# Values of heads 0 and 1 made together, with 512 moving columns and a new order

## The chip, the cores and the metric

The kernel runs on one core of a Trainium2 chip. Its metric is the device time of one execution in microseconds (us). Five engines work side by side, each through its own instructions in order: PE (TensorE, matrix products; PEld is its weight load), DVE (VectorE), ACT (ScalarE), POOL (GpSimd) and SP (SyncE, which here issues all DMA transfers).

## What is computed

One layer of an encoder trunk on 1024 tokens with 1024 features, float32. Only the start matters here: a norm, one input projection, and gated linear attention with four heads in both directions.

```python
h = rmsnorm(x, norm_mix)                       # x: (1024 tokens, 1024 features)
q, k, v, r, lr_f, lr_b, u, g_a, g_b = split(h @ w_in)
                                               # q, k: 4 heads of 128; v: 4 heads of 256
log_a = log_sigmoid(lr @ w_decay_up + b_decay) / 16        # one for each direction
# per head, in chunks: decayed keys and queries, scores inside a chunk times v,
# and a state S = decay * S + k^T v carried from chunk to chunk, forward and backward
o = gla(q, k, v, log_a_f) + gla_backward(q, k, v, log_a_b)
...                                            # norm per head, gates, pooling, merge, FFN, norm
```

## The kernel before

**Products in three parts.** Every float32 operand of the large products is split into a high part and a rest: `split_to` (L196) copies the source to the high part on ACT (L197) and subtracts it on DVE or POOL (L198). `mm3` (L273) then issues three matmuls (high by high, high by rest, rest by high) into one PSUM bank and calls `pump`. A step of `mm3` with 512 moving columns counts as one unit, one with 256 as half a unit.

**What is interleaved, and how.** The order of all instructions is fixed while the program is written, and `pump` (L158) is the clock of that: generators wait in the list `side`, and each `pump` takes the units from the first of them and runs its next step when its delay is used up. So a generator's instructions come between two products of the main line, at a place set by counted units and not by time. `pending` holds weight splits (one for every two units), and `aside` holds jobs that prepare later weights (`prepare_beside`, one job for every so many units, POOL operations with DMA transfers).

**The main line of the first 390 us.** Tokens are in eight tiles of 128. `norm_x` norms a tile and then issues the load of the tile four ahead; `to_features` transposes two tiles on PE (L318), applies the gain on ACT (L325, tile `hh`) and takes the rest on DVE (L328, `hl`). `values(w, v, t)` (L384) makes the values of one head for one token tile: the token tile is the stationary operand, the 256 columns of the weights move, 24 matmuls. Before, the values of head 0 for all eight tiles come first, with the norms and transposes of the later tiles between them; then the low-rank product for the decays (L449) for both token halves; then queries and keys of head 0 (`project_qk`, four products of eight units, weights stationary, 512 tokens moving); then, for heads 1 to 3, queries and keys and after them the values of eight tiles (32 units each). After head 3 comes the section that makes `r` (L996 on), 128 units.

**Attention beside it.** `attention(h)` is a generator that is put in line once the head's queries and keys are made, and it runs beside the next products. Its steps, with delays in units, are: four decay products `z` (L641), Exp and Ln on ACT (L650, L656); then four times a decay (DVE: L663 `la`, a scan L670 or L675, L678/L671, L681), its exponentials (ACT, L688 to L690) and its application to the keys (DVE L696, POOL L697 and L698), 4.4 units apart; key transposes `kp` (L714), split into `kt` by ACT and DVE; then seven backward state updates `advance` 1.2 units apart (PE `kv`, DVE `st` L726 or L728, DVE `so` L733, ACT `sb` L780); scores (L741); and eight output steps with the forward state. The fourth update of the backward chain still uses the first `kt`; the fifth is the first that needs the second one. The generator of the next head starts when the one before it has ended; an attention is 59 to 60 units long. `normalize` (L834) scales the outputs of the head before, eight DVE operations after the Exps of the next head.

**Buffers.** 39 slots of one tile size in SBUF are shared by nearly everything; PSUM has three banks for the main products and five for the rest. Raw weights have four buffers.

Of the kernel before, what the change touches and what calls it, by code (L numbers as in the profile page):

```python
# [17 lines left out]
P = 128  # L18
# [33 lines left out]
def kernel(  # L52
# [38 lines left out]
    def name(s):  # L91
        count[0] += 1
        return f"{s}_{count[0]}"
# [92 lines left out]
    def begin(gen, delay=0.0):  # L186
        side.append([gen, delay])
# [47 lines left out]
    order = []  # L235
    for h in range(HEADS):
        cols_of = [(Q0 + h * DK, DK), (K0 + h * DK, DK), (V0 + h * DV, DV)]
        order += [(w_in, KT, *c) for c in (cols_of if h else cols_of[2:] + cols_of[:2])]
    order += [(w_in, KT, R0 + j * P, P) for j in range(KT)]
    order = iter(order)  # L240
    loaded, ready = [], []
# [72 lines left out]
    def transpose_tile(ps, xt, i, kp):  # L314
        for kk in range(2):
            c = slice((2 * kk + i) * P, (2 * kk + i + 1) * P)
            k = 2 * kp + kk
            nc.tensor.transpose(ps[:, c], xt[:, k * P : (k + 1) * P], ident[:, :])  # L318

    def gain_and_split(ps, kp, t0, act, gain):  # L320
        c = slice((t0 % 4) * P, (t0 % 4 + 2) * P)
        both = range(2 * kp, 2 * kp + 2)
        srcs = [(ps[:, i * 2 * P : (i + 1) * 2 * P], gain[:, k : k + 1]) for i, k in enumerate(both)]
        for k, (src, g) in zip(both, srcs):
            nc.scalar.activation(act(k, t0 // 4)[0][:, c], src, AF.Copy, scale=g)  # L325
        for k, (src, g) in zip(both, srcs):
            hi, lo = act(k, t0 // 4)
            nc.vector.scalar_tensor_tensor(  # L328
                lo[:, c], src, g, as_f32(hi[:, c]), op0=ALU.mult, op1=ALU.subtract
            )  # L330
# [19 lines left out]
    def load_x(t):  # L350
        nc.sync.dma_start(xt[t % 4][:, :], x[t * P : (t + 1) * P, :])
# [4 lines left out]
    def load_up(i, d, w):  # L356
        r = 2 * RANK * i + RANK * d
        nc.sync.dma_start(uraw[r : r + RANK, :, d, :], w[0].rearrange("r (h c) -> r h c", h=HEADS))

    load_x(0)  # L360
    load_rows(0, *vec_rows[0])
    load_x(1)
    for i in range(1, len(vec_rows)):
        load_rows(sum(n for _, n in vec_rows[:i]), *vec_rows[i])
    fetch()
    for t in (2, 3):
        load_x(t)
    nc.sync.dma_start(lraw[:, :, :], w_in[:, LR0:U0].rearrange("(k p) c -> p k c", p=P))
# [35 lines left out]
    def value_slots():  # L404
        return [(slot(F32R, (4, DV), "vh"), slot(F32R, (4, DV), "vl")) for _ in range(2)]

    v = value_slots()
    norm_x(0)

    vps = bank(ps_g, "vps")  # L410
# [7 lines left out]
    for t in range(2):  # L418
        for kp, ps in enumerate(trs):
            transpose_tile(ps, xn[t], t, kp)  # L420
    prepare()
    for kp, ps in enumerate(trs):
        pending.pop(0)()
        gain_and_split(ps, kp, 0, hT, g_mix)
    w = take(ahead=False)
    norm_x(2)
    norm_x(3)
    for t in range(0, NT, 2):
        if t + 4 < NT:
            begin(norms(t + 4), 1)  # L430
        if t == 2:
            for d, w_up in enumerate((w_decay_up_fwd, w_decay_up_bwd)):
                for i in range(4):
                    load_up(i, d, w_up)
        values(w, v, t)
        finish_side()
        if t + 2 < NT:
            begin(to_features(xn[(t + 2) % 4 :], t + 2, hT, g_mix), 0.5)
        values(w, v, t + 1)
        finish_side()  # L440
        if t == 4:
            low_rank_weights()
    prepare()
    lrT = slot(F32R, (2, HALF), "lrT")
    for half in range(2):
        ps = bank(ps_mm)
        for k in range(KT):
            for i in range(2):
                nc.tensor.matmul(  # L449
                    ps[:, :], lw[k // 4][:, k % 4, :, :].rearrange("p a r -> p (a r)"), hT(k, half)[i],  # L450
                    start=k == 0 and i == 0, stop=k == KT - 1 and i == 1,
                )
            pump(2 / 3)
        nc.scalar.copy(lrT[:, half, :], ps[:, :])
        nc.vector.tensor_tensor(lrT[64:96, half, :], ps[64:96, :], as_f32(lrT[64:96, half, :]), op=ALU.subtract)
# [175 lines left out]
    def attention(h, q, k):  # L631


        qe = [slot(s="qe") for _ in range(2)]
        ke = [slot(s="ke") for _ in range(2)]
        fac = {}
        runs = ((1, 1), (0, 1), (0, 0), (1, 0))
        zs, las = {}, {}
# [43 lines left out]
            totals[half, d] = tot  # L682

        def exponentials(half, d):
            cs, tot, e_q = zs[half, d], totals[half, d], qe[half]
            f = vec(12, "fac")
            sign = INV_NORMALIZER if d == 0 else -INV_NORMALIZER
            nc.scalar.activation(e_q[:, d, :], cs[:, :], AF.Exp, scale=sign)  # L688
            nc.scalar.activation(cs[:, :], cs[:, :], AF.Exp, scale=-sign)
            nc.scalar.activation(f[:, :8], tot[:, :], AF.Exp, scale=INV_NORMALIZER)  # L690
            fac[half, d] = f

        def apply_decay(half, d):
            f, e_q, e_k = fac[half, d], qe[half], ke[half]
            f2 = f[:, :8].rearrange("p (n a) -> p n a", a=2)
            nc.vector.tensor_tensor(e_k[:, d, :], zs[half, d][:, :], k[:, half, :], op=ALU.mult)  # L696
            nc.gpsimd.tensor_tensor(e_q[:, d, :], e_q[:, d, :], q[:, half, :], op=ALU.mult)  # L697
            nc.gpsimd.tensor_tensor(f[:, 8:], f2[:, :, 0], f2[:, :, 1], op=ALU.mult)  # L698
# [146 lines left out]
    def load_o(h):  # L845
        o_heads[h] = [slot(shape=(4, DV), s="ol") for _ in range(2)]
        for half in range(2):
            nc.sync.dma_start(o_heads[h][half][:, :, :], o_out[h][:, 4 * half : 4 * half + 4, :])

    for h in range(HEADS):  # L850
        qk = project_qk()
        begin(attention(h, *qk))
        if h == 0:
            prepare_beside(map(branch_jobs, range(4)), 6)
        if h > 0:
            v = value_slots()
            w = take()
            for t in range(NT):
                values(w, v, t)
        v_heads[h] = v  # L860

    class Unit:

# [1006 lines left out]
```

## Time and profile before

| | us |
|---|---|
| timed runs, median of 3 | 1399.0 (1397.69 to 1401.03) |
| the profiled execution, its span | 1400.4 |
| PE busy in it | 1371.4 (98%) |
| DVE / ACT / POOL busy | 854.4 / 624.6 / 750.4 |

The profile gives no time of its own for the profiled execution beside its span; its span lies within the range of the timed runs, 1.4 us above their median. The lines of the profile name the kernel's lines (L271 is the matmul in `products`), and an operation is written as output tile <- input tiles; the moving operand of a matmul stands first. "Idle before" is the time for which the engine had nothing to do just before an instruction, with what it waited for.

### The profile page before, as it was taken

The numbers are of one execution on the slowest core, as the hardware profiler recorded it, in microseconds if no ns is written. First come the engines' busy times: TensorE is split into PE (matmuls) and PEld (weight loads), VectorE is DVE, ScalarE is ACT, GpSimd is POOL, SyncE is SP. The second block draws the span as 40 slices with busy tenths as digits, with TensorE's granted clock in tenths as the row PEclk, the third lists the DMA queues.
The fourth block names the chain that finished last, engine by engine and source line by source line (L and its number), as shares of the span: only waits on it lengthen the run. The fifth ranks groups of instructions, "written<-read, shape, count | busy, mean of one in ns | idle before, by whom it ended". The sixth has DMA issues, their size and how long they took to land.

```text
span 1400.4 us, 18571 instructions
## 1 busy us (share of the span) xinstructions
PE 1371.4 (98%) x6677; PEld 1157.4 (83%) x6677; DVE 854.4 (61%) x1073; ACT 624.6 (45%) x1119; POOL 750.4 (54%) x558
## 2 busy tenths in 40 slices
PE   7999999999999999999999999999999999999997
PEld 6889898988888878788887888888888888888876
DVE  6256857677745975587874865556565556343363
ACT  6364655554334444455346633333333334453253
POOL 3251616132288456468665176666666667454354
PEclk9999999999999999999999999999999999999999
DMA  6212413222368667996524455554444447975461
GB/s 193 76 45 61 136 59 107 89 79 71 125 207 286 199 220 235 346 407 233 194 76 173 173 180 174 173 173 156 145 142 148 140 153 255 388 255 218 165 234 67
DMA packets 167612, 243.62 MB, mean 174 GB/s; under 512 B 10936, under 2 KB 98016, under 8 KB 167520
## 3 DMA queue, kind: packets, MB, share of 16 engines
q1 hardware_dynamic: 167520, 242.45, 51.2%
q8 instruction: 52, 0.85, 0.2%
q14 instruction: 40, 0.33, 0.1%
HBM read 164.55 MB, written 77.86 MB: 173 GB/s over the span
## 4 chain that ended last, share of the span: by engine, by line
PE 81%; DVE 7%; ACT 4%; issue 3%; POOL 2%; DMA 2%; SPq 0%; POOLq 0%; DVEq 0%; ACTq 0%
PE ps L271 73%; PE op L813 2%; POOL wl L198 1%; PE kv L271 1%; PE sc L741 1%; PE op L271 1%; DVE z L670 1%; PE yb L271 1%; PE tr L318 1%; PE ps L449 1%; PE tp L972 1%; DMA gor<-g_out 0%; DMA wor<-t_out 0%; DVE z L675 0%; DMA u_out<-uph 0%
## 5 line engine op out<-in xcount | busy, mean ns | idle before, releaser
L198 POOL TENSOR_TENSOR wl<-fs,wh 128x512 fp32r<-128x512 f32 x120 | 165.9, 1386 | 163.4 <-ACT wh L197 138.1
L271 PE MATMUL ps<-gl,wh 128*128 128x512 f32 x616 | 239.8, 389 | 0.9 <-DVE gl L1462 0.9
L271 PE MATMUL ps<-gh,wh 128*128 128x512 f32 x616 | 240.4, 390 | 0.0
L271 PE MATMUL ps<-gh,wl 128*128 128x512 f32 x616 | 239.7, 389 | 0.0
L198 POOL TENSOR_TENSOR wl<-fraw,wh 128x512 fp32r<-128x512 f32 x90 | 129.1, 1435 | 63.9 <-ACT wh L197 63.9
L271 PE MATMUL ps<-hh,wh 128*128 128x512 f32 x376 | 150.4, 400 | 0.0
L198 POOL TENSOR_TENSOR ol<-gor,oh 128x1024 fp32r<-128x1024 f32 (+1 forms) x42 | 100.3, 2394 | 93.1 <-ACT oh L197 86.0
L271 PE MATMUL ps<-hh,wl 128*128 128x512 f32 x376 | 146.9, 391 | 0.0
L271 PE MATMUL ps<-hl,wh 128*128 128x512 f32 x376 | 146.8, 390 | 0.0
L198 POOL TENSOR_TENSOR wl<-raw,wh 128x512 fp32r<-128x512 f32 x47 | 64.4, 1382 | 152.8 <-ACT wh L197 141.4
L271 PEld LDWEIGHTS ps<-gl,wh 128*128 128x128 f32 x616 | 115.7, 188 | 25.0 <-DVE gl L1462 1.3
L271 PEld LDWEIGHTS ps<-gh,wl 128*128 128x128 f32 x616 | 115.7, 188 | 24.2
L271 PEld LDWEIGHTS ps<-gh,wh 128*128 128x128 f32 x616 | 115.7, 188 | 23.6
L271 PE MATMUL ps<-oh,oh 128*128 128x512 f32 x308 | 119.9, 389 | 1.3 <-DVE x L1792 1.3
L271 PE MATMUL ps<-ol,oh 128*128 128x512 f32 x308 | 119.9, 389 | 0.2 <-DVE ol L198 0.2
L271 PE MATMUL ps<-oh,ol 128*128 128x512 f32 x308 | 119.8, 389 | 0.0
L198 POOL TENSOR_TENSOR wl<-wraw,wh 128x512 fp32r<-128x512 f32 x56 | 90.9, 1653 | 45.4 <-ACT wh L197 36.1
L198 DVE TENSOR_TENSOR ol<-wor,oh 128x1024 fp32r<-128x1024 f32 (+1 forms) x42 | 62.0, 1496 | 53.9 <-ACT oh L197 46.6
L197 ACT CAST wh<-fs 128x512 fp32r<-128x512 f32 x120 | 73.8, 615 | 28.4 <-DVE fs L882 28.3
L271 PEld LDWEIGHTS ps<-hh,wl 128*128 128x128 f32 x376 | 70.8, 188 | 15.3
L271 PEld LDWEIGHTS ps<-hl,wh 128*128 128x128 f32 x376 | 71.1, 189 | 13.5
L271 PEld LDWEIGHTS ps<-hh,wh 128*128 128x128 f32 x376 | 71.1, 189 | 13.2
(251 smaller groups left out, 3197.4 us busy)
## 6 DMA issues: line engine op xcount, KB each, us to landing
fraw<-in_w_ffn_in_dram SPq DMA_DIRECT2D x44, 512.0 KB, 6.1
gor<-g_out SPq DMA_DIRECT2D x35, 512.0 KB, 6.3
raw<-in_w_in_dram SPq DMA_DIRECT2D x48, 256.0 KB, 3.1
g_out<-s SPq DMA_DIRECT2D x44, 256.0 KB, 2.3
fraw<-in_w_in_dram SPq DMA_DIRECT2D x20, 512.0 KB, 6.5
wor<-t_out SPq DMA_DIRECT2D x20, 512.0 KB
g_out<-g SPq DMA_DIRECT2D x33, 256.0 KB, 2.6
x<-in_x_dram SPq DMA_DIRECT2D x16, 512.0 KB, 4.9
```

The costliest lines, as they stand in the source:

```text
L197: nc.scalar.copy(hi, src)
L198: eng.tensor_tensor(lo, src, as_f32(hi), op=ALU.subtract)
L271: nc.tensor.matmul(ps, a[i], b[j], start=first and n == 0, stop=last and n == 2, skip_group_check=onto)
L318: nc.tensor.transpose(ps[:, c], xt[:, k * P : (k + 1) * P], ident[:, :])
L449: nc.tensor.matmul(ps[:, :], lw[k // 4][:, k % 4, :, :].rearrange("p a r -> p (a r)"), hT(k, half)[i], start=k == 0 and i == 0, stop=k == ...
L670: nc.vector.tensor_tensor_scan(cs[:, :], cy, la[:, :], 0.0, op0=ALU.mult, op1=ALU.add)
L741: nc.tensor.matmul(sc[d][:, i * CH : (i + 1) * CH], chunk_of(ke, n, d), chunk_of(qe, n, d), start=True, stop=True,)
L813: nc.tensor.matmul(op[:, :DV], a, b, start=False, stop=j == len(terms) - 1)
L972: nc.tensor.transpose(tp[:, i * P : (i + 1) * P], o_heads[j // 2][half][:, i, (j % 2) * P : (j % 2 + 1) * P], ident[:, :],)
```

## The change

Three things change together.

1. The values of heads 0 and 1 are made in one product of 512 moving columns (256 for each head) by `pair_products`, for which 8 weight tiles of 128 rows by 512 columns are loaded one at a time (`load_pair_weight`) and kept split in slots (`split_pair_weight`, ACT with DVE and POOL in turn). Before, the weights of one head were four transfers of 256 rows by 256 columns.
2. The order is new. Tiles 0 and 1 come first, both within each step over the features; their steps also issue the splits of the weights, the gains and the norms of tiles 2 and 3 (`first_steps`). Then tile 2, tile 3, and head 0's queries and keys by token halves (`first_qk`): low-rank product, queries and keys for the first half, while the tiles of the second half are normed and transposed, then the same for the second. Then `attention(0)` is put in line, and tiles 4, 5 and (6, 7) follow beside it. Head 1 has no values of its own any more. Heads 2 and 3 are as before.
3. The slots `qe` and `ke` of an attention are taken when they are first written, and the jobs beside the products come every 5 units and not every 6, beginning 32 units later.

In PE's program there are 192 matmuls fewer; from the last part of the `r` section on, the order of PE's instructions is the same as before.

```diff
-        order += [(w_in, KT, *c) for c in (cols_of if h else cols_of[2:] + cols_of[:2])]
+        order += [(w_in, KT, *c) for c in cols_of[: 2 if h < 2 else 3]]
...
+    def load_pair_weight():
+        k = len(pair_raw)
+        raw = wts.tile([P, HALF], F32, tag="raw", name=name("vraw"), bufs=4)
+        nc.sync.dma_start(raw[:, :], w_in[k * P : (k + 1) * P, V0 : V0 + 2 * DV])
+        pair_raw.append(raw)
+
+    def split_pair_weight():
+        k = len(pair_w)
+        w = slot(F32R, s="wv")
+        pair_w.append((w[:, 0, :], w[:, 1, :]))
+        split_to(*pair_w[k], pair_raw[k][:, :], (nc.vector, nc.gpsimd)[k % 2])
+        if len(pair_raw) < KT:
+            load_pair_weight()
...
-    fetch()
+    for _ in range(4):
+        load_pair_weight()
     for t in (2, 3):
         load_x(t)
...
+    def pair_products(ts, before=None):
+        banks = [bank(ps_mm) for _ in ts]
+        for k in range(KT):
+            if before:
+                before(k)
+            for ps, t in zip(banks, ts):
+                mm3(ps[:, :], tokens(hT(k, t // 4), t), pair_w[k], k == 0, k == KT - 1)
+        for ps, t in zip(banks, ts):
+            for h in range(2):
+                if t % 4 == 0:
+                    pair_v[h].append((slot(F32R, (4, DV), "vh"), slot(F32R, (4, DV), "vl")))
+                split_to(*(part[:, t % 4, :] for part in pair_v[h][t // 4]), ps[:, h * DV : (h + 1) * DV])
+
+    def first_steps(k):
+        if k % 2 == 0:
+            gain_and_split(trs[k // 2], k // 2, 0, hT, g_mix)
+        if k < KT - 1:
+            split_pair_weight()
+        if k in (3, 5):
+            norm_x(k // 2 + 1)
+        if k == 6:
+            begin(to_features(xn[2:], 2, hT, g_mix), 0.5)
+
+    split_pair_weight()
+    pair_products((0, 1), first_steps)
+    finish_side()
+    fetch()
+    begin(norms(4), 1)
...
+    pair_products((2,))
+    finish_side()
+    begin(to_features(xn, 4, hT, g_mix), 1)
+    low_rank_weights()
     prepare()
-    for kp, ps in enumerate(trs):
...
-    w = take(ahead=False)
-    norm_x(2)
-    norm_x(3)
-    for t in range(0, NT, 2):
...
-        values(w, v, t)
...
+    pair_products((3,))
+    finish_side()
...
+    def first_qk():
+        q, k = slot(s="q"), slot(s="k")
+        begin(norms(6), 1)
+        low_rank(0)
+        weights = [take()]
+        begin(to_features(xn[2:], 6, hT, g_mix), 1)
+        for half in range(2):
+            if half:
+                finish_side()
+                low_rank(1)
+                prepare()
+            for n, (dst, scale) in enumerate(((q, DK**-0.5), (k, 1.0))):
+                if n == len(weights):
+                    weights.append(take(ahead=False))
+                ps = feature_major(weights[n], hT, half)
+                nc.scalar.activation(dst[:, half, :], ps[:, :], AF.Copy, scale=scale)
+        return q, k
+
     for h in range(HEADS):
-        qk = project_qk()
+        qk = project_qk() if h else first_qk()
         begin(attention(h, *qk))
         if h == 0:
-            prepare_beside(map(branch_jobs, range(4)), 6)
-        if h > 0:
+            for ts in ((4,), (5,), (6, 7)):
+                pair_products(ts)
+            v_heads.update(enumerate(pair_v))
+            prepare_beside(map(branch_jobs, range(4)), 5)
+        if h > 1:
             v = value_slots()
             w = take()
             for t in range(NT):
                 values(w, v, t)
-        v_heads[h] = v
+            v_heads[h] = v
```

More of the change, by code (lines that the diff above doesn't have):

```diff
@@ L358, in load_up @@
         nc.sync.dma_start(uraw[r : r + RANK, :, d, :], w[0].rearrange("r (h c) -> r h c", h=HEADS))
+    pair_raw, pair_w = [], []
+    def load_pair_weight():
[10 more added lines that the diff above has]
+            load_pair_weight()
     load_x(0)
@@ L405, in value_slots @@
         return [(slot(F32R, (4, DV), "vh"), slot(F32R, (4, DV), "vl")) for _ in range(2)]
-    v = value_slots()
     norm_x(0)
@@ L420, with low_rank @@
             transpose_tile(ps, xn[t], t, kp)
-    prepare()
-    for kp, ps in enumerate(trs):
-        pending.pop(0)()
-        gain_and_split(ps, kp, 0, hT, g_mix)
-    w = take(ahead=False)
-    norm_x(2)
-    norm_x(3)
-    for t in range(0, NT, 2):
[L429 to L434, printed above, removed]
-        values(w, v, t)
[L436 to L443, printed above, removed]
+    pair_v = [[], []]
+    def pair_products(ts, before=None):
[24 more added lines that the diff above has]
+    begin(norms(4), 1)
+    for d, w_up in enumerate((w_decay_up_fwd, w_decay_up_bwd)):
+        for i in range(4):
+            load_up(i, d, w_up)
+    pair_products((2,))
+    finish_side()
+    begin(to_features(xn, 4, hT, g_mix), 1)
+    low_rank_weights()
+    prepare()
+    pair_products((3,))
+    finish_side()
     lrT = slot(F32R, (2, HALF), "lrT")
-    for half in range(2):
+    def low_rank(half):
         ps = bank(ps_mm)
@@ L631, in attention @@
     def attention(h, q, k):
-        qe = [slot(s="qe") for _ in range(2)]
-        ke = [slot(s="ke") for _ in range(2)]
+        qe, ke = {}, {}
         fac = {}
@@ L684, in exponentials @@
         def exponentials(half, d):
+            if half not in qe:
+                qe[half] = slot(s="qe")
             cs, tot, e_q = zs[half, d], totals[half, d], qe[half]
@@ L693, in apply_decay @@
         def apply_decay(half, d):
+            if half not in ke:
+                ke[half] = slot(s="ke")
             f, e_q, e_k = fac[half, d], qe[half], ke[half]
```

## The prediction

> **What bounds the kernel now.** I read the page first: the span, PE's share, and the chain of work that ended last.
>
> ```profile
> span 1400.4 us, 18571 instructions
> PE 1371.4 (98%) x6677; PEld 1157.4 (83%) x6677; DVE 854.4 (61%) x1073; ACT 624.6 (45%) x1119; POOL 750.4 (54%) x558
> PE 81%; DVE 7%; ACT 4%; issue 3%; POOL 2%; DMA 2%; SPq 0%; POOLq 0%; DVEq 0%; ACTq 0%
> ```
>
> PE is the bound. A change in PE's own work counts in full; anything else counts where PE waits for it. So I go through the stretch that the diff touches, up to the `r` section, and look for PE's work there and for its waits. The PE work is read from the chain of waits in order of time (start, us, how many):
>
> ```profile
> 24.04 3.59 PE ps L271 x30
> 27.63 0.44 PE tr L318 x4
> 45.08 7.28 PE ps L449 x32
> 52.36 22.44 PE ps L271 x99
> ```
>
> 30 matmuls of 256 columns took 3.59 us, 119.7 ns each; 99 of 512 took 22.44 us, 226.7 ns each. From 24.04 us PE runs without a break until head 0's attention begins at 52.36 + 22.44 = 74.8 us. What is left at 24.04 us confirms it: 3 matmuls of tile 1 and 6 tiles of 24 (147 x 0.1197 = 17.6), 8 groups of transposes (3.5), the low-rank product (7.28), queries and keys (22.44), together 50.8 us.
>
> **Columns.** 384 matmuls of 256 columns become 192 of 512: 192 x (2 x 119.7 - 226.7) ns = 2.4 us less PE work, half of it ahead of head 0's attention and half beside it. The Trainium skill, "TensorE: Matmul & The Clock Gate", Back-to-back issue gap, gives N/2.4 + 2.5 ns for a warm matmul; by that 256 columns take 109.2 ns and 512 take 215.8 ns, and the estimate from it would be a gain of 0.5 us alone. The trace has 119.7 and 226.7, 11 ns more for each instruction, and decides.
>
> **The start.** Views: the timeline by engine, and the windows (PE, PEld, DVE, ACT, POOL busy, granted clock, DMA share, GB/s).
>
> ```profile
> 8.72 10.19 SPq L351 DMA_DIRECT2D x<-in_x_dram  x4
> 17.96 1.06 ACT L311 ACTIVATE xn<-x 128x1024 f32<-128x1024 f32 x1 [0.15 <-DMA x<-in_x_dram]
> 3.00:4.00 1.00, 0.00 (x0) 0.00 (x0) 1.00 (x3) 0.00 (x0) 0.90 (x2) 1.00 0.99 361
> 12.99 0.65 ACT L197 CAST wh<-raw 128x512 fp32r<-128x512 f32 x1
> 13.50 0.88 ACT L325 ACTIVATE hh<-tr,cols 128x256 fp32r<-128x256 f32 x2
> 14.23 1.10 ACT L311 ACTIVATE xn<-x 128x1024 f32<-128x1024 f32 x1
> 15.27 1.09 ACT L311 ACTIVATE xn<-x 128x1024 f32<-128x1024 f32 x1
> 15.45 0.15 DVE L302 TENSOR_SCALAR n1rs<-n1ms 128x1 f32<-128x1 f32 x1 [0.16 <-ACT xn L311]
> 16.27 0.75 DVE L307 TENSOR_SCALAR xn<-x,n1rs 128x1024 f32<-128x1024 f32 x1 [0.66 <-POOL n1rs L303]
> 14.42 0.88 DVE L328 SCALAR_TENSOR_TENSOR hl<-tr,cols,hh 128x256 fp32r<-128x256 f32 x2 [0.37 <-ACT hh L325]
> 11.22 3.79 POOL L198 TENSOR_TENSOR wl<-raw,wh 128x512 fp32r<-128x512 f32 x3 [2.99 <-ACT wh L197]
> 10.69 0.56 PE L271 MATMUL ps<-wh,hh 128*128 128x256 f32 x1
> ```
>
> The first pair (tiles 0 and 1) now wants 2 MB of weights instead of 1 MB. Four of its eight tiles take the places of the old four transfers. The fifth waits for a raw buffer, and in SP's order it stands behind the loads of token tiles 4 and 5 (issued 8.72 us on). Tile 5 landed at 17.9 us (ACT then stopped waiting for it), so the fifth weight tile comes 256 KB / 361 GB/s = 0.7 us later: 18.7 us. The next three follow every 0.7 us, ahead of their use. Token tiles 6 and 7 and head 0's weights come behind them, some 15 us before they are needed: nothing.
>
> Before that PE has four steps of 6 matmuls, 5.4 us of work, from 10.7 us on and partly at a low clock: done at about 17.2. Then, in ACT's order: cast at 18.7, the square of tile 2 at 19.2 (casts start 0.51 apart, squares 1.04), gains at 20.25. PE's fifth step begins at 20.8. Its third matmul wants `hl`, which on DVE stands behind the norm of tile 2: the sum of squares is there at 20.4, `xn` starts 0.8 later and takes 0.75, half of the `hl` pair 0.45: 22.45 us. From there PE has 22 matmuls (5.0) and four groups of transposes (1.8): it would be done at 29.2 at full clock. POOL's splits (1.3 each) and the second norm stay just ahead of it. The clock:
>
> ```profile
> 12.77:16.18 3.41, 2.95 (x20) 2.43 (x20) 1.93 (x6) 3.41 (x7) 2.73 (x3) 1.00 1.06 350
> 16.18:19.59 3.41, 1.57 (x12) 1.24 (x12) 1.99 (x5) 3.05 (x8) 1.16 (x3) 1.00 0.48 149
> 19.59:23.00 3.41, 3.41 (x19) 3.41 (x17) 2.75 (x8) 1.62 (x5) 0.55 (x1) 0.50 0.73 229
> 227.80:231.20 3.40, 1.31 (x6) 0.84 (x6) 2.15 (x3) 2.59 (x6) 2.55 (x3) 1.00 0.29 77
> 231.20:234.60 3.40, 3.20 (x11) 2.81 (x12) 3.23 (x6) 1.02 (x2) 3.32 (x4) 0.50 0.20 77
> ```
>
> A stretch of 3.4 us in which PE was busy for 1.57 or 1.31 us is followed by one at clock 0.50; one with 2.95 is not. With the same stretches, the changed start has 1.0 busy in 16.18 to 19.59 and about 1.4 in the next: half clock to 26.4 us. That takes 2.0 us: done at 31.2. I take this; 29.2 is the low end. Then follow 48 matmuls (10.9), transposes (3.5), the low-rank product, queries and keys: 44.1 us. Two norm chains are now close behind PE. Tiles 6 and 7 are squared only when tile 3's values are cast, and two squares (2.1), scaling (0.8 + 0.75, partly twice) and casts make about 5 us, while PE has the low-rank half and one step, 4.3 us: 0.7 us of waiting (0 to 1.5). Head 0's attention begins at 31.2 + 44.1 + 0.7 = 76.0 us, **1.2 us later** than before (73.3 to 77: 1.5 earlier to 2.2 later), its share of the 2.4 us included.
>
> **Beside the attention.** Tiles 4 to 7 take 96 x 226.7 ns = 21.8 us where 192 x 119.7 ns = 23.0 stood: **-1.2 us**. What else changes is which products lie beside which step. PE's waits of that stretch, and DVE's and ACT's rows that lead to them:
>
> ```profile
> 95.85 0.69 DVE L198 TENSOR_TENSOR kt<-kp,kt 128x512 fp32r<-128x512 f32 x1 [1.98 <-ACT kt L197]
> 103.72 0.69 DVE L198 TENSOR_TENSOR kt<-kp,kt 128x512 fp32r<-128x512 f32 x1 [1.15 <-ACT kt L197]
> 104.32 0.41 DVE L198 TENSOR_TENSOR vl<-ps,vh 128x256 fp32r<-128x256 f32 x1
> 104.73 0.28 PE L271 MATMUL kv<-vh,kt 128*128 128x256 f32 x1
> 146.07 0.69 DVE L663 TENSOR_TENSOR la<-la,z 128x512 f32<-128x512 f32 x1 [1.85 <-ACT z L656]
> 164.62 0.69 DVE L198 TENSOR_TENSOR kt<-kp,kt 128x512 fp32r<-128x512 f32 x1 [0.64 <-ACT kt L197]
> 166.72 0.28 PE L271 MATMUL kv<-vh,kt 128*128 128x256 f32 x1
> 206.85 2.05 ACT L656 ACTIVATE z<-z 128x512 f32<-128x512 f32 x4
> 209.23 0.42 DVE L198 TENSOR_TENSOR vl<-ps,vh 128x256 fp32r<-128x256 f32 x1 [3.23 <-ACT vh L197]
> 209.57 0.68 DVE L663 TENSOR_TENSOR la<-la,z 128x512 f32<-128x512 f32 x1
> 227.99 0.38 PE L271 MATMUL kv<-vh,kt 128*128 128x256 f32 x1 [0.25 <-DVE st L726]
> 231.40 0.58 PE L271 MATMUL kv<-vh,kt 128*128 128x256 f32 x1 [2.10 <-DVE kt L198]
> 295.75 0.39 PE L271 MATMUL kv<-vh,kt 128*128 128x256 f32 x1 [1.04 <-DVE kt L198]
> ```
>
> In each head the fifth state update is the first to need the second `kt`. In head 0 it was ready at 104.4 for 104.73, 0.3 to spare; in head 1 at 165.3 for 166.72, 1.4 to spare. In heads 2 and 3 PE waited for it.
>
> *Head 2.* DVE could have begun its first decay with the first Ln, at 207.5; it stood for 3.23 us before the rest of the last value tile (209.23), whose cast ACT had behind all four Ln. In head 1 nothing stood there. The price: 0.25 + 2.10 us, and then 3.4 us at half clock, 1.7: 4.0 us. Now head 1's attention is put in line only at unit 64 and not at 32, so it starts 4 to 6 units later than the end of head 0's would let it, and all later ones move with it. In the program's order head 2's attention now has no value split between its Exps and its first decay, as head 1's had none: **-4.0 us** (0 if the scans, not the split, made the lag).
>
> *Head 0.* New in DVE's order: two splits (tile 5) behind the first decay, and four (tiles 6 and 7) between the fourth decay and the first state update. DVE had 1.98 us idle ahead of the first `kt`, which covers the two. The four take 4 x 0.41 = 1.6 us and delay the second `kt`; between the first key transposes and the fifth update stand 33 matmuls of 512 where 9 of 512 and 48 of 256 stood, 7.5 us for 7.8, so PE comes 0.3 earlier: 1.6 + 0.3 - 0.3 = **+1.6 us**. A wait of that size leaves 1.8 us busy, between the 1.57 that brought a half clock and the 2.95 that didn't; with it 3.3 to 4.0, and 0 if scans run freer while fewer weights are split beside them.
>
> *Head 1* lies as head 0 did, against the values of head 2: 0. *Head 3* still has one value tile behind its Ln, where before there were two; of its 1.04 us I take off half: **-0.5** (-1.0 to +3.0, head 2's price before).
>
> `qe` and `ke` taken later cost nothing: the slots they now take were last read by the first steps of the last pair, units earlier. From the last part of `r` on PE's order is unchanged, and the gain is carried on.
>
> **Sum:** 1.2 - 1.2 - 4.0 + 1.6 - 0.5 = -2.9 us. Against the profiled execution, 1400.4, that is 1397.5; it lies 1.4 above the median of the runs, 1399.0, which gives **1396.1 us**. About 2.8 us (0.2%) is what a measurement here can tell from no change, so the forecast lies at that bound.
>
> **Rivals.**
> *The wait moves from head 2 to head 0.* The four splits bring the whole wait with the half clock there, 4.0 instead of 1.6: -0.5 us, 1398.5. For it: `kt` had only 0.3 us to spare. Against: tile 5's splits are covered, and few weights are split on POOL then.
>
> *The scans decide, and it gets slower.* How long a scan takes varies by a factor of two:
>
> ```profile
> L675 DVE TENSOR_TENSOR_SCAN z<-la,carry x8: 1229/1670/2341, 85.2 to 280.6; 128x511 f32<-128x511 f32 x8
> L670 DVE TENSOR_TENSOR_SCAN z<-carry,la x8: 1231/1776/2277, 91.4 to 289.7; 128x512 f32<-128x512 bf16 x8
> ```
>
> The branch jobs now come every 5 units and not every 6, so POOL works more beside these heads. If that stretches the four scans of a head by more than 0.35 us each (1.4 to spare in head 1; from 1.7 to over 2.0 us), PE waits there. Head 2 then keeps its 4.0 and head 0 gets 4.0: 1.2 - 1.2 + 4.0 - 0.5 = +3.5, 1402.5; head 1 as well, 1406.5. The Trainium skill, "SBUF — State Buffer", Who interferes with whom, has a VectorE instruction with two SBUF inputs shut out while GpSimd reads SBUF; for the scans, whose result lies in PSUM, the spread of 1.23 to 2.34 us agrees.
>
> *No half clock in the start* is the low end above: 2.0 us less, 1394.1. That the change doesn't do what it says is no rival: PE's program has 192 matmuls fewer.
>
> **How the numbers follow.** The forecast has 0.53 (its own range 1392.5 to 1399, with the start at either clock and head 0 from 0 to 3.3), the moved wait 0.25, the scans 0.22. The forecast case is faster by over 0.2% in about eight of ten, the moved wait rarely, the scans never: faster 0.47. Within 0.2%: most of the moved wait and some of the forecast, 0.28. Slower: the scans and a rest, 0.25. The range 1392.0 to 1403.0 takes the forecast's own and the scans with two heads.
>
> **What would show it.** PE idle from about 17 to 21 us with ACT's cast of the fifth weight tile starting at 18.7; the granted clock 0.50 in one or two stretches behind it; the first `z` at 76; no PE wait over 0.5 us for `kt` in head 2, one of 1 to 2 us in head 0. Wrong would be: a first `z` past 78, a wait for `kt` in head 1, or head 2's wait unchanged although no value split stands ahead of its first decay.

## The result: slower by 0.4%, and the profile after

| | median, us | runs | lowest to highest |
|---|---|---|---|
| before | 1399.37 | 6 | 1397.69 to 1402.18 |
| after | 1404.13 | 6 | 1403.81 to 1406.19 |

The ratio is 1.0043 with a 95% interval of 1.0028 to 1.0058: 4.8 us slower. The forecast was 1396.1 us, with a range up to 1403.0. It was wrong in sign, and the time lies outside the range.

The page of the changed kernel's profiled execution (this run took 1404.11 us, 1.7 more than its span):

```profile
span 1402.4 us, 18182 instructions
PE 1367.1 (97%) x6485; PEld 1143.3 (82%) x6485; DVE 857.7 (61%) x1076; ACT 624.6 (45%) x1119; POOL 744.3 (53%) x555
```

PE has 192 instructions and 4.3 us of busy time less, but the span is 2.0 us longer: what was taken out of PE's work came back as waiting. Two rows of PE's timeline in each kernel, the first `z` of head 0 and the first `tp` of the `r` section, behind which PE's order is the same in both, cut the span into three. After, then before:

```profile
77.67 0.39 PE L674 MATMUL z<-lrT,up 128*128 128x512 f32 x1
337.74 0.49 PE L1030 MATMUL tp<-ident,ol 128*128 128x128 f32 x3
```

```profile
74.64 0.39 PE L641 MATMUL z<-lrT,up 128*128 128x512 f32 x1
```

| | before | after | difference | forecast |
|---|---|---|---|---|
| up to the first `z` | 74.6 | 77.7 | +3.0 | +1.2 |
| from there to the first `tp` (334.1 before) | 259.4 | 260.1 | +0.6 | -4.1 |
| the rest | 1066.3 | 1064.7 | -1.7 | 0 |

The last row is no work of the change: before, one stretch of 3.4 us at clock 0.50 lay at 569 us, where the changed kernel's execution has none.

The start, in windows (us, PE, PEld, DVE, ACT, POOL busy, granted clock, DMA share, GB/s), and the rows of the timeline at the end of PE's hole:

```profile
14.80:18.21 3.41, 1.86 (x9) 1.20 (x7) 0.00 (x0) 0.00 (x0) 0.00 (x0) 1.00 1.01 384
18.21:21.63 3.42, 0.73 (x2) 0.30 (x2) 1.57 (x4) 3.24 (x7) 0.82 (x2) 1.00 0.09 32
21.63:25.04 3.41, 2.94 (x7) 2.38 (x8) 2.74 (x7) 2.45 (x6) 2.60 (x3) 0.50 0.50 154
```

```profile
18.39 0.62 ACT L197 CAST wv<-vraw 128x512 fp32r<-128x512 f32 x1 [5.60 <-DMA vraw<-in_w_in_dram]
20.47 0.73 PE L271 MATMUL ps<-wv,hh 128*128 128x512 f32 x2 [3.81 <-ACT hh L325]
36.98 0.44 PE L318 MATMUL tr<-ident,xn 128*128 128x128 f32 x2 [0.28 <-DVE n1rs L302]
38.46 0.44 PE L318 MATMUL tr<-ident,xn 128*128 128x128 f32 x2 [1.04 <-DVE xn L307]
50.63 0.44 PE L318 MATMUL tr<-ident,xn 128*128 128x128 f32 x2 [1.06 <-DVE xn L307]
```

The cast of the fifth weight tile and the hole came nearly as foretold (18.7 and 17.2 to 20.8 us), with one stretch at half clock behind it. The last three rows were not: PE also waits for the norms of tiles 4 and 5 (1.3 us), and of 6 and 7 (1.1 us, ending at 50.6). That is 2.4 us of idle time, 2.7 counted from start to start of the matmuls, where the forecast had 0.7.

PE's waits between 80 and 330 us, grouped by what it waited for (total, times, longest), after and then before:

```profile
PE kv L271 <- DVE kt L198: 3.7, 3, 1.4
PE kv L271 <- ACT vh L197: 1.9, 1, 1.9
PE op L271 <- DVE p L198: 0.2, 1, 0.2
```

```profile
PE kv L271 <- DVE kt L198: 3.4, 3, 2.1
PE kv L271 <- DVE st L726: 0.2, 1, 0.2
PE op L271 <- DVE p L198: 0.2, 1, 0.2
```

The rows behind these, one for each of heads 0, 1 and 2:

```profile
104.27 0.38 PE L271 MATMUL kv<-vh,kt 128*128 128x256 f32 x1 [1.92 <-ACT vh L197]
175.95 0.39 PE L271 MATMUL kv<-vh,kt 128*128 128x256 f32 x1 [1.42 <-DVE kt L198]
240.07 0.39 PE L271 MATMUL kv<-vh,kt 128*128 128x256 f32 x1 [1.20 <-DVE kt L198]
```

Before, heads 0 and 1 had no such wait. Head 2's got shorter, but did not go; head 3's is as before (1.06 us, 1.04 before). The expectations below count a wait from start to start of two matmuls beyond their pitch (2.08, 1.58, 1.36), which is about 0.16 more than the idle time in a row.

### The profile page after: what moved, and what is told of

Its sections match the earlier page's. It is cut to its first block, busy times and chain, and to the rows that moved or that the text cites. A ratio compares the mean times of both kernels' runs of the same rounds, so it can differ in the third digit from the quotient of the medians.

```text
span 1402.4 us, 18182 instructions
## 1 busy us (share of the span) xinstructions
PE 1367.1 (97%) x6485; PEld 1143.3 (82%) x6485; DVE 857.7 (61%) x1076; ACT 624.6 (45%) x1119; POOL 744.3 (53%) x555
## 5 line engine op out<-in xcount | busy, mean ns | idle before, releaser
L198 POOL TENSOR_TENSOR wl<-raw,wh 128x512 fp32r<-128x512 f32 x40 | 54.4, 1370 | 129.5 <-ACT wh L197 119.1
```

Of the source, the lines that this page charges most:

```text
L198: eng.tensor_tensor(lo, src, as_f32(hi), op=ALU.subtract)
```

## The experiments

Each is the changed kernel with one edit, unless it says otherwise. All times, with the ratio to the kernel before in runs on the same chip, and the median of the kernel before in those runs:

| | median, us | lowest to highest | ratio | 95% interval | kernel before, us |
|---|---|---|---|---|---|
| loads of tiles 4 and 5 later (e_start) | 1400.42 | 1398.44 to 1403.13 | 1.0016 | 1.0003 to 1.0028 | 1398.70 |
| norms earlier (e_norms) | 1401.55 | 1400.29 to 1404.06 | 1.0025 | 1.0013 to 1.0037 | 1398.70 |
| stores of outputs later (e_flush) | 1401.77 | 1400.46 to 1402.78 | 1.0020 | 1.0007 to 1.0032 | 1398.70 |
| tiles in the order 4, 7, 6, 5 (e_order0) | 1403.58 | 1402.85 to 1406.74 | 1.0039 | 1.0027 to 1.0052 | 1398.70 |
| 256 columns again (e_c256) | 1403.45 | 1402.18 to 1406.31 | 1.0032 | 1.0020 to 1.0044 | 1399.52 |
| jobs every 6 units (e_every6) | 1409.06 | 1406.37 to 1411.18 | 1.0068 | 1.0049 to 1.0086 | 1399.52 |
| the first three together (all3) | 1393.88 | 1392.62 to 1395.26 | 0.9959 | 0.9946 to 0.9973 | 1399.52 |
| and tile 4 ahead (all3_t4) | 1392.79 | 1390.86 to 1394.23 | 0.9951 | 0.9937 to 0.9965 | 1399.52 |
| and tiles 4, 5 ahead (all3_t45) | 1390.69 | 1389.26 to 1391.72 | 0.9946 | 0.9934 to 0.9959 | 1398.65 |
| all3_t4 with 256 columns (all3_t4_c256) | 1396.49 | 1394.73 to 1397.51 | 0.9986 | 0.9977 to 0.9995 | 1398.65 |
| the kernel before, stores later (before_flush) | 1397.07 | 1394.87 to 1398.28 | 0.9986 | 0.9977 to 0.9995 | 1398.65 |

The changed kernel's 1404.13 us stands against 1399.37 for the kernel before. The times below come from three chips, on which the kernel before differs by up to 0.9 us; so a gain against the changed kernel is given as the difference of the two medians, and in brackets as the difference of their distances to the kernel before. A ratio has an interval of about 1.7 us to either side, so a gain under about 2 us is not shown by the times alone.

### The hole in the start

```diff
 def norm_x(t):
-        if t + 4 < NT:
+        if 2 <= t and t + 4 < NT:
             load_x(t + 4)
 def split_pair_weight():
         if len(pair_raw) < KT:
             load_pair_weight()
+            if len(pair_raw) == KT:
+                load_x(4)
+                load_x(5)
```

> The changed kernel with one difference: the loads of token tiles 4 and 5 are issued behind the eighth weight tile and not ahead of the fifth. Theory A (the order of the transfers makes the hole in the start): in the changed kernel PE stood still for 3.97 us at 16.3 us, and ACT's cast of the fifth weight tile began at 18.39 us. 1 MB less ahead of that tile at about 360 GB/s is 2.9 us: the cast begins at 15.5, PE's hole is about 1.2 us, no stretch of 3.4 us has PE busy for less than 2 us, so none is at clock 0.50 (that one cost 1.7), and the first z comes 4.5 us earlier, at 73.2 instead of 77.7. Time 1399.6 us (from 1404.1). Theory B (the free raw buffers decide, not the order): the hole stays at 3 to 4 us and the time at 1404. Theory C (gain lost to late tiles): the hole shrinks, but PE waits longer for tiles 4 and 5 before their transposes, 3 us and more instead of 1.5; time 1401 to 1403.

Measured: 3.7 us faster than the changed kernel (3.0). The first `z` comes at 73.39 us, 4.3 earlier, and the cast of the fifth weight tile at 15.02. The same windows in this kernel:

```profile
14.80:18.21 3.41, 3.15 (x14) 2.25 (x12) 1.52 (x4) 3.19 (x7) 0.76 (x2) 1.00 0.97 327
18.21:21.63 3.42, 2.89 (x12) 2.18 (x12) 2.75 (x7) 2.51 (x6) 2.62 (x3) 1.00 0.72 265
21.63:25.04 3.41, 3.24 (x21) 2.70 (x21) 1.64 (x5) 1.68 (x4) 0.99 (x1) 1.00 0.65 223
```

PE is busy for 3.15 and 2.89 us where it had 1.86 and 0.73, and no half clock follows there. (In this execution, the slowest of the ten, one came later, at 101.9 us, behind head 0's wait.) Theory A holds: 1 MB of token tiles, wanted only at 34 us, stood in SP's order ahead of weights wanted at 16 us. The waits for the norms stayed as they were, so C is out.

### The norms

```diff
 def first_steps(k):
+        if k == 7:
+            norm_x(4)
+            norm_x(5)
...
-    begin(norms(4), 1)
+    begin(norms(6), 1)
...
 def first_qk():
-        begin(norms(6), 1)
         low_rank(0)
```

> The changed kernel with the norms one place earlier: tiles 4 and 5 in the last step of the first pair (ACT was idle there from 24.1 to 27.2 us), tiles 6 and 7 beside tile 2's products. Theory A (PE's waits ahead of the transposes of tiles 4 to 7, 0.44 + 1.10 and 1.12 us, come from ACT's order: the squares stand behind the casts of the values): all three go, the first z comes 2.7 us earlier, at 75.0, and the time is 1401.4 us. Theory B (the transposes would then wait for something else, for example for the gains of the tiles before, which the squares now delay): 1 to 2 us come back as other waits between 24 and 55 us, time 1402.5 to 1404.

Measured: 2.6 us faster (1.9), near what A has. Between 24 and 80 us PE has no wait left that the profile shows. The first `z` comes at 76.1 us and not at 75.0, since this execution had two stretches at half clock behind the hole and not one. The changed kernel has, between 24 and 80 us,

```profile
PE tr L318 <- DVE xn L307: 2.1, 2, 1.1
PE tr L318 <- DVE n1rs L302: 0.3, 1, 0.3
```

### The stores of the outputs

```diff
 def attention(h, q, k):
         yield 3.5
-        flush()
...
         apply_decay(1, 1)
+        flush()
         yield HOLD - 2
```

> The changed kernel with the two stores of a head's outputs issued some 13 units later in the next head's attention, behind the loads of the value weights of heads 2 and 3 and not ahead of them. Theory A (a late transfer in front of the exponentials): in heads 1 and 2 ACT stood 3.1 and 3.4 us waiting for a raw weight tile whose load was queued behind these stores (the first store waited until DVE had scaled the outputs, at 151.3 us), and the exponentials and everything behind them on DVE came that much later. Without it ACT's waits for that transfer fall under 1 us, PE's waits for kt of 1.58 us (head 1) and 1.36 us (head 2) go or fall under 0.4 us, and the time is 1401.2 us. Theory B (DVE's scans are stretched by POOL, my rival before the run): ACT's waits for the transfer may go, but PE's waits for kt stay at 1.2 us and more in both heads; time 1404 us. Theory C (one of them only: the loads of head 2 stand behind 1 MB of other weights anyway): head 1's wait goes, head 2's stays, 1402.5 us.

Measured: 2.4 us faster (1.7), and in heads 1 and 2 PE's waits for `kt` are gone (0.9 us in all is left, in head 3, where there were 3.7). This is the chain in the changed kernel, in head 1: SP's queue, then ACT, then DVE.

```profile
151.35 2.42 SPq L499 DMA_DIRECT2D o_out<-o  x2
154.73 2.18 SPq L205 DMA_DIRECT2D raw<-in_w_in_dram  x4
```

```profile
159.25 0.62 ACT L197 CAST wh<-raw 128x512 fp32r<-128x512 f32 x1 [3.06 <-DMA raw<-in_w_in_dram]
159.88 1.28 ACT L723 ACT_TABLE_LOAD   x1
161.18 0.60 ACT L723 ACTIVATE qe<-z 128x512 f32<-128x512 f32 x1
```

```profile
148.10 5.31 DVE L871 TENSOR_SCALAR o<-o,ors 128x256 f32<-128x256 f32 x8
158.96 0.43 DVE L714 TENSOR_TENSOR z<-z,tot 128x256 f32<-128x256 f32 x1
162.30 0.69 DVE L733 TENSOR_TENSOR ke<-z,k 128x512 f32<-128x512 f32 x1 [2.91 <-ACT z L724]
175.20 0.69 DVE L198 TENSOR_TENSOR kt<-kp,kt 128x512 fp32r<-128x512 f32 x1 [1.14 <-ACT kt L197]
```

The stores wait in SP's queue until DVE has scaled the outputs. The four loads of the next value weights stand behind them and are issued only at 154.7. ACT has the cast of the first of them ahead of the exponentials of the first decay and stands for 3.06 us. DVE then waits 2.91 us for those exponentials, and the second `kt` comes that much later. In the kernel with the stores later the loads are issued from 145.2 us on, and the same cast and exponential are

```profile
156.95 0.61 ACT L197 CAST wh<-raw 128x512 fp32r<-128x512 f32 x1
158.88 0.60 ACT L722 ACTIVATE qe<-z 128x512 f32<-128x512 f32 x1
```

with no wait, although that execution began head 0's attention 0.9 us later. So A, and B is out: in head 1 the four scans took 6.29 us together here, more than the 5.94 of the changed kernel, and PE did not wait. POOL has a part in the chain all the same, at its head: DVE's scaling, for which the stores wait, took 5.31 us beside POOL and 2.18 in the kernel before (last section). What a faster scaling alone would give was not tried.

### More or less work on POOL

```diff
-            prepare_beside(map(branch_jobs, range(4)), 5)
+            prepare_beside(map(branch_jobs, range(4)), 6)
```

> The changed kernel with the jobs beside the products every 6 units again, as in the kernel before, and not every 5. Theory A (PE's waits for kt in heads 1 and 2 come from a transfer in front of ACT's exponentials): 1.58 and 1.36 us stay within 0.6 of that, time 1403.5 to 1404.7 us. Theory B (POOL's extra work beside DVE makes them, by longer scans): both fall under 0.4 us, time 1401.2 us.

Measured: 4.9 us slower (4.8), which neither theory had. The rows tell why (SP's queue, then ACT, then PE):

```profile
154.51 1.20 SPq L615 DMA_DIRECT2D s_out<-wsum  x2
155.82 1.31 SPq L533 DMA_DIRECT2D wsum<-in_w_branch_gla_dram  x2
157.24 3.02 SPq L205 DMA_DIRECT2D raw<-in_w_in_dram  x4
```

```profile
163.44 0.62 ACT L197 CAST wh<-raw 128x512 fp32r<-128x512 f32 x1 [7.71 <-DMA raw<-in_w_in_dram]
```

```profile
167.24 0.65 PE L751 MATMUL kp<-ident,ke 128*128 128x128 f32 x4 [3.31 <-DVE ke L733]
```

At the other rate two loads of 512 KB for the jobs fall ahead of the value weights in SP's queue. ACT waits 7.71 us for the same cast, PE 3.31 us for the first keys and 1.0 more for the second `kt`, and a stretch at half clock follows. Head 2's wait for `kt` is gone in the same run; why is not shown. So the other rate did not help. It does not settle theory B, since it moved the transfers too (the run with the stores later does, above). But A as I wrote it was too narrow, since it is the whole queue in front of that cast that counts. Three kernels (stores later, changed, jobs every 6) give ACT's wait and PE's wait in head 1: none and none, 3.06 and 1.42, 7.71 and 4.3 us.

### Head 0: the order of the last tiles

```diff
-            for ts in ((4,), (5,), (6, 7)):
+            for ts in ((4,), (7,), (6,), (5,)):
```

> The changed kernel with the products beside head 0's attention in the order tile 4, 7, 6, 5, one at a time, instead of 4, 5, (6 and 7 together). Theory A (the first state update waits for its values): PE stood 2.08 + 0.39 us ahead of the first kv of head 0, whose values (tile 7) were cast by ACT behind tile 6's second cast, which waited for DVE's subtraction of tile 6's first half, behind the fourth decay. With tile 7 made two tiles earlier the wait falls under 0.5 us, tiles 6 and 5 are there when their updates want them, and the time is 1402.0 us. Theory B (my prediction's reason: the splits between the fourth decay and the first update delay the second kt): the wait moves to the fifth update and is 1.0 to 1.6 us there; time 1403.0 to 1403.7 us.

Measured: 0.5 us faster (0.1 slower), which the runs don't tell from nothing; the wait for the values is gone, and one for `kt` stands at the fifth update:

```profile
110.07 0.39 PE L271 MATMUL kv<-vh,kt 128*128 128x256 f32 x1 [2.09 <-DVE kt L198]
```

In the changed kernel the first state update waits for its values. ACT and DVE there (changed kernel):

```profile
99.65 0.38 ACT L197 CAST vh<-ps 128x256 fp32r<-128x256 f32 x1 [0.28 <-PE ps L271]
103.57 0.65 ACT L197 CAST vh<-ps 128x256 fp32r<-128x256 f32 x2 [3.55 <-DVE vl L198]
```

```profile
102.79 0.43 DVE L714 TENSOR_TENSOR z<-z,tot 128x256 f32<-128x256 f32 x1
103.13 0.41 DVE L198 TENSOR_TENSOR vl<-ps,vh 128x256 fp32r<-128x256 f32 x1
```

ACT casts head 0's half of tile 6, and the cast of head 1's half waits until DVE has subtracted the first half, which stands behind the fourth decay; the cast of tile 7, which the first update wants, stands behind that. (Each of the four tiles has such a wait of ACT for DVE, 5.6 us in all, though the two halves are different columns of the bank.) Theory A's place was right. But the second `kt` is later than B has it (2.1 us, where B had 1.0 to 1.6), hidden behind the first wait, so removing one shows the other.

### Columns alone

The order of the changed kernel, with two products of 256 columns for each of tiles 2 to 7:

```diff
 def pair_products(ts, before=None):
         banks = [bank(ps_mm) for _ in ts]
+        for h, k in () if before else [(h, k) for h in range(2) for k in range(KT)]:
+            c = slice(h * DV, (h + 1) * DV)
+            for ps, t in zip(banks, ts):
+                mm3(ps[:, c], tokens(hT(k, t // 4), t), tuple(w[:, c] for w in pair_w[k]), k == 0, k == KT - 1)
+        for k in range(KT if before else 0):
...
```

> The changed kernel with the values of tiles 2 to 7 made in products of 256 columns, head 0's half of the bank and then head 1's, in the same order of tiles (tiles 0 and 1 stay at 512): 144 matmuls more. Theory A (the columns gain what the two pitches say): 144 x (2 x 119.7 - 226.7) ns = 1.8 us more work on PE, in a stretch in which PE is the bound: 1405.9 us against 1404.1, and 24 matmuls of 256 columns beside 12 of 512 show 119.7 and 226.7 ns each. Theory B (a cost of 10 ns for each instruction only shows where weights change, and a matmul that keeps its columns short is hidden under its weight load): no difference, 1404.1. The Trainium skill, TensorE: Matmul & The Clock Gate, Back-to-back issue gap, gives N/2.4 + 2.5 ns; by that the difference would be 0.4 us.

Measured: 1403.45 us, 0.7 less than with 512 columns (0.8), which the runs don't tell from nothing, though 144 matmuls were added. The pitch is what A says: from one row to the next here are three matmuls, in 0.35 to 0.36 us, 0.12 us each.

```profile
32.70 0.28 PE L271 MATMUL ps<-wv,hl 128*128 128x256 f32 x1
33.05 0.28 PE L271 MATMUL ps<-wv,hl 128*128 128x256 f32 x1
33.41 0.28 PE L271 MATMUL ps<-wv,hl 128*128 128x256 f32 x1
```

PE's waits for the attention between 80 and 340 us in this kernel are

```profile
PE kv L271 <- DVE kt L198: 2.2, 2, 1.1
PE kv L271 <- ACT vh L197: 0.9, 1, 0.9
```

2.5 us less than in the changed kernel. Of that, 1.0 lies in head 0, beside which 96 of the 144 added matmuls lie: the time from its first `z` to head 1's grew by 0.6 us (66.6 to 67.2) for 1.2 us of added work. So about half of that work took the place of waiting. (The edit also finishes head 0's half of a tile before head 1's, which can shorten that wait by itself.) The other 1.5 lie in heads 1 and 2, whose products are the same in both kernels; why PE waits less there is not shown. The same edit where few waits are left:

> The three edits and tile 4 ahead, with the values of tiles 2 to 7 in products of 256 columns (144 matmuls more, 1.8 us more PE work by the pitches). In the changed kernel the same step cost nothing, since PE's waits shrank by what its work grew. Here few waits are left (0.41 and 1.75 us, both in head 0, beside which half of these products lie). Theory A (the gain of 512 columns is real, and shows where PE does not wait): 0.9 to 1.8 us slower, 1393.7 to 1394.6 us against 1392.8. Theory B (512 columns gain nothing, whatever the waits): 1392.4 to 1393.2 us.

Measured: 1396.49 us, 3.7 more than all3_t4 (4.6), more than either theory had. It decides between neither, since two other things came with the edit and are as large as the difference; so A's 1.8 us, worked out from the pitches of the rows, is not shown as time. By the rule of the Trainium skill, "TensorE: Matmul & The Clock Gate", Back-to-back issue gap, the estimate for the added work is 0.4 us. In the start, with head 0's half of tile 2 first, PE runs through the eight feature steps twice as fast and waits 1.5 us more for `hl` (2.6 us in all, where all3_t4 has 1.1), and 0.9 us for `hh` at 17 us; the first `z` comes 2.5 us later. And behind head 0's wait for `kt` this execution has a stretch at half clock (112.6 us), which all3_t4's has not: 1.7 us, half of its length.

### Together

> The changed kernel with three edits together: the loads of tiles 4 and 5 behind the eighth weight tile (alone 1400.4 us), the norms of tiles 4 to 7 one place earlier (alone 1401.6), the stores of a head's outputs behind the value weights of the next heads (alone 1401.8). Theory A (three waits that have nothing to do with each other): the gains of 3.7, 2.5 and 2.3 us add up, 1395.6 us, and PE's only waits over 0.5 us up to 340 us are those of about 1 us in the first steps, 2.5 us in head 0 and 1.2 us in head 3. Theory B (one gives way to another: tiles 4 and 5 arrive at 18 to 20 us and their squares are now wanted at about 21): a new wait of 1 to 2 us before the transposes of tiles 2 to 5, 1396.6 to 1397.6 us.

Measured: 1393.88 us, 1.7 us better than the sum. One reason at hand is the clock: the executions of the three single edits had one or two stretches at half clock before the end. Here PE's granted clock does not fall before the end of this kernel's execution. No new wait came up: behind the first steps, up to 340 us, the waits over 0.3 us are 1.9 us for `vh` in head 0 and 0.9 for `kt` in head 3.

```diff
         qk = project_qk() if h else first_qk()
+        if h == 0:
+            pair_products((4,))
         begin(attention(h, *qk))
...
-            for ts in ((4,), (5,), (6, 7)):
+            for ts in ((5,), (6, 7)):
```

> The three edits together, and the values of tile 4 made ahead of head 0's attention (then tile 5, then 6 and 7 together beside it). The last splits come 8 units earlier against the attention's steps, ahead of the fourth decay. Theory A (in head 0 PE waits because the splits of tiles 6 and 7 stand behind or among the decays): the 2.5 us ahead of head 0's first state update go, at most 0.5 us is left in the whole head, 2 us less than with the three edits alone: 1393.6 us. Theory B (the wait moves to the fifth update and its second kt, as with the order 4, 7, 6, 5): 1.5 to 2.3 us there, no gain, 1395.6 us.

Measured: 1392.79 us. The wait moved to the second `kt` (1.6 us), so B. The 1.1 us gained are less than the runs tell apart; head 3's wait, 0.9 us, is gone in this execution.

> The three edits, and the values of tiles 4 and 5 both ahead of head 0's attention (6 and 7 together beside it). With tile 4 alone ahead, PE still waited 0.41 and 1.75 us in head 0, the second time for the second kt. Theory A (splits among the decays make DVE late): the four splits of tiles 6 and 7 now come before or with the first decay, where DVE was idle while ACT worked on Exp and Ln, so the two waits fall under 0.6 us together: 1391.2 us against 1392.8. Theory B (the decays themselves take that long: scans of 1.9 to 2.3 us there): the wait for the second kt stays at 1.2 us and more, 1392.3 to 1393 us.

Measured: 1390.69 us (`pair_products((5,))` ahead of the attention as well). A: in heads 0 and 1 PE waits no more, and from 80 to 330 us there are only

```profile
PE op L856 <- ACT sf L855: 0.8, 1, 0.8
PE kv L271 <- DVE kt L198: 0.3, 1, 0.3
```

The gain on all3_t4 (2.1 us; 1.2) is less than the runs tell apart, so A rests on the waits. This kernel is 0.54% faster than the one before (0.41 to 0.66), and 13.4 us faster than the changed kernel (12.7), with the same matmuls.

### The kernel before

> The kernel before with the stores of a head's outputs issued some 13 units later, the edit that alone gave 2.3 us in the changed kernel. Theory A (in the kernel before no exponential stood behind a late transfer; ACT waited 1.2 us in all for weights in the three attentions): no difference, within 0.7 us of the kernel before. Theory B (the stores are in the way in any order): 1.5 to 2.5 us faster, 1396.9 to 1397.9 us.

Measured: 1.6 us faster than the kernel before (0.14%, 0.05 to 0.23). A is out: the stores were in the way before, too. Head 2 there has one wait of

```profile
229.78 0.38 PE L271 MATMUL kv<-vh,kt 128*128 128x256 f32 x1 [1.38 <-DVE kt L198]
```

where it had 0.25 and 2.10. So 1.0 of head 2's 2.4 us went with the transfers, and 1.4 stayed, with the value split still ahead of the first decay; that it is the split was not tried by itself. Since the stores cost the kernel before something too, the fair measure of the change with its reorderings is this kernel: all3_t45 is 6.4 us faster, on the same chip. Moving norms was not tried on the kernel before.

## Why the prediction was wrong

Up to the first `tp` the forecast had -2.9 us and the two executions differ by +3.7 (334.1 to 337.7 us): 6.6 us apart. By terms of the forecast that is the start 1.8, head 1 1.4, head 2 1.1, head 3 0.5, head 0 0.3, and 1.4 that was not found. The main steps that failed are the norms in the start, taken at 0.7 us, and head 1, taken at 0 without a look at SP's queue.

- **Columns, -2.4 us: right as work, not confirmed as time.** The pitches were as foretold. PE's busy time fell by 4.3 us in all, but two stretches at half clock fewer are part of that. Between the first `z` and the first `tp` it fell by 1.5 us (255.6 to 254.1), where the columns (1.2) and head 2's half clock (1.7) make 2.9. With the columns undone the time did not rise, and beside head 0 about half of the added work took the place of waiting. So the sentence that a change in PE's own work counts in full failed too, in the half beside the attention.
- **The start, +1.2: right in mechanism, one term mis-sized.** The cast of the fifth tile came at 18.39 (18.7), the hole and the half clock behind it came too, and the first pair was done at 30.3 (31.2). The waits for the norms measured 2.7 and not 0.7: I followed the chain of tiles 6 and 7 and not that of tiles 4 and 5, whose squares stand behind the casts of the first pair's values. The half clock was put at 2.0 us, where 3.4 us at half speed hold back 1.7. I also took the hole as given, when 3.7 us of it (3.0) hung on the order of two loads.
- **Head 2, -4.0: partly.** Its waits fell from 2.4 to 1.2 us, and the half clock there (1.7) went. What was left came from the loads behind the stores, which the prediction did not look at: with the stores later it is gone. Of the moves the prediction followed DVE's order, not SP's queue.
- **Head 1, 0: wrong.** It measured 1.42 us. "Lies as head 0 did" was argued from PE's units. But ACT's cast of the first value weight moved from behind the first exponentials (151.97 us after 149.84 in the kernel before) to ahead of them, and its load stands behind stores that wait for DVE. "A wait for `kt` in head 1" was among the signs named for being wrong.
- **Head 0, +1.6: size near, place wrong; the size is luck.** 1.92 us for the values of the first update, since ACT's second cast waits for DVE's first subtraction. The delay of the second `kt` that I had in mind is there behind it.
- **Head 3, -0.5:** its wait is unchanged, about 1.0 us.
- **Own time against the median.** I took the span, 1400.4, for the time. With the 1.7 us around it that execution took 1402.1, 2.7 above the median and not 1.4, and its three stretches at half clock are part of that. In the sum this cancels, since the forecast is the median 1399.0 less 2.9 either way. But a half clock that only some executions have (head 2's 1.7) was no gain to count in full.
- **The rival "the scans decide"** gave 1402.5 to 1406.5, and the time lies there, but not by its reason: the four scans of head 1 took 1.23, 1.23, 1.73 and 1.75 us, less than before in sum (5.9 after 6.5).

Summed over heads, the measured changes (columns -1.2, head 0 +1.9, head 1 +1.4, head 2 -2.9, head 3 0) make -0.8 us between the first `z` and the first `tp`; +0.6 was measured. The other 1.4 us are not in PE's idle time, which grew by 2.1 us (3.8 to 6.0), as these waits say; they are the busy time that did not fall, and their cause stays open.

## What to carry to other kernels

When a change shifts one interleaved stream against another, write down for each queue (SP's too) what now stands ahead of what, and follow each load to the instruction that waits for it: a cast of weights in front of an unrelated exponential makes every transfer queued before it part of the critical chain. Work saved on the busiest engine is a gain only in stretches where that engine does not already wait; look for its waits first. And try the cheap reorderings (a load later, a norm earlier, a store later, two tiles ahead) before judging the idea: with them the same change went from 0.43% slower to 0.54% faster.

## What the runs showed of the hardware

- **Time and granted clock go together.** In 30 runs of the kernel before on one chip the mean granted clock was 0.999 where the time was 1395.8 to 1397.4 us, and 0.996 or 0.997 where it was above 1400.1: stretches of 3.41 us at half speed come in some executions and not in others, and by their length each can hold PE back by about 1.7 us. A stretch in which PE was busy for 0.73 of 3.42 us was followed by one; stretches with 2.89 and 3.15 were not. Between 1.5 and 1.8 us both happen: the wait in head 0 brought a half clock in the kernel with tiles 4 and 5 loaded later (first row), and none in the one with the stores later (second row), where PE was even less busy:

```profile
98.51:101.92 3.41, 1.78 (x11) 1.41 (x11) 2.42 (x7) 1.12 (x4) 0.00 (x0) 1.00 0.00 1
101.72:105.13 3.41, 1.49 (x7) 0.91 (x5) 2.87 (x6) 0.65 (x2) 0.00 (x0) 1.00 0.46 137
```

- **DVE's scaling beside POOL.** The eight scalings of 128x256 in the chain above took 5.31 us together, those of the kernel before 2.18 us; three of the eight ran beside POOL's work:

```profile
142.04 2.18 DVE L834 TENSOR_SCALAR o<-o,ors 128x256 f32<-128x256 f32 x8
```

POOL worked from 148.6 us on in the changed kernel, and had nothing to do at that place before. The Trainium skill, "SBUF — State Buffer", Who interferes with whom, says that such a one-input VectorE operation can enter a mode in which it and GpSimd block each other for whole instructions; the trace agrees, with 0.35 us for one scaling before POOL began and 1.38 to 1.40 for each of the three beside it.
